# Half-column matrix products of a gated-linear-attention and a state-space layer, gathered into one row per head and per group

## The chip, the cores and the metric

One core of a Trainium2 chip runs the whole kernel in one launch. The metric is the device time of one execution in microseconds, the median of three runs. One more execution was recorded by the hardware profiler; all rows below come from it.

## The reference, cut to what matters

Two layers work on 1024 tokens of width 1024 in float32. Each has an RMS norm in front, one wide input projection, a token mixer, a SiLU gate, an output projection and a residual add.

Layer 0 (GLA) has 4 heads, key width 128, value width 512. With `b` the running sum of the log gates inside a chunk it computes

```
attn = sum(q[i] * k[j] * exp(b[i] - b[j]))        # j <= i, over the 128 key channels
o    = (q * exp(b)) @ S  +  attn @ v
S    = exp(b_last) * S   +  (k * exp(b_last - b)).T @ v
```

Layer 1 (SSD, Mamba-2) has 8 groups of 4 heads of 64 columns and a state of 128; with `a` the running sum of decays

```
y = ((C @ B.T) * exp(a[l] - a[s])) @ xdt  +  (C @ h) * exp(a)  +  x * D      # s <= l
h = exp(a_last) * h + B.T @ (xdt * exp(a_last - a))
```

Gate and norm follow in both (`o = rmsnorm(o) * silu(g)`; `y = rmsnorm(y * silu(z))`), and a last norm ends the trunk.

## The kernel before

Time is cut into two blocks of 512 tokens; the program runs GLA block 0, GLA block 1, SSD block 0, SSD block 1. A chunk inside a block is 128 tokens, so a block has four (`NC`). Wide projections are done in three `fp32r` products (high by high, high by low, low by high; lines 223 to 225, and 468 to 470 for the values). They are cut into units of 12 products of 512 columns; every unit needs a piece of weight, cast by ScalarE (line 171) and, at its first use, split by GpSimd (line 176), which is the case in block 0 of either layer.

Beside the units run side programs, the mixers, one per head or group. They are Python generators; after every unit a mixer is moved on by about one `yield`. This gives a priority; a scheduler then sets each engine's final order from a timeline of its own. The order is fixed once built: on the chip an engine that reaches an instruction whose data are late stops there.

The GLA mixer of a head makes `attn` in pieces, with exponents that stay small: products at three scales `s` of 16, 4 and 1 rows, and one of 64 rows. `keys(s)` and `queries(s, ...)` (lines 574 to 604) build the scaled operands on VectorE and ScalarE, two halves per scale. `products` (line 606) multiplies them, the two halves of a chunk into PSUM partitions 0 to 63 and 64 to 127: each product uses 64 of TensorE's 128 columns. `place` (line 617) copies the parts into `a64` by masks, from there they go to `at`, and line 699 multiplies `at` by `v`. Line 640 is the 64-row product. The operand of the gate has 96 rows, three copies of 32 (lines 429 to 432), and line 539 multiplies it with `wup`, also 96 rows.

The SSD mixer of a group has four heads in two halves `i`. `decays` and `exps` (lines 909 and 923) make the decay matrices `M` on ScalarE, two lines on VectorE multiply them by `cbm` (lines 1033 and 1060), and `outputs(i, M)` (line 931) makes `po` from the carried state (line 936, all 128 columns) and `py` from `xdt` and `M` (line 941, 64 columns each: head 0 of a half into partitions 0 to 63, head 1 into 64 to 127). `gated` reads both from PSUM. `M` and the broadcast decays share six buffers (`v`). Line 268, in the small projections `gk` and `dt`, uses 32 of the columns.

An `fp32` product of these lines leaves two records in the trace, an `fp32r` product one: the 8 products of a half in line 941 are `x16`.

PSUM has four banks for projections (`pp`) and four for mixers (`mb`). Engine names: `V` VectorE (DVE), `A` ScalarE (ACT), `G` GpSimd (POOL), `PE` TensorE.

Of the kernel before, what the change touches and what calls it, by code (L numbers as in the profile page):

```python
# [10 lines left out]
F32 = mybir.dt.float32  # L11
# [5 lines left out]
P = 128  # L17
# [36 lines left out]
def hybrid_kernel(ctx: ExitStack, tc: tile.TileContext, xT, w_in0, w_gk, w_up, w_out0,  # L54
# [16 lines left out]
    def tl(tag, bufs, shape=(P, T), dt=F32):  # L71
        cnt[0] += 1
        return sb.tile(list(shape), dt, name=f"{tag}_{cnt[0]}", tag=tag, bufs=bufs)
# [335 lines left out]
    class Gla:  # L409
# [13 lines left out]
        def gk(self):  # L423
            def evac(o):

                low = o
                if self.raw:
                    V.tensor_tensor(low, o, self.r[0][0:32, :], op=ALU.mult)
                st = tl("stp", 2, (96, T), F32R)
                V.tensor_copy(st[0:32, :], low)  # L430
                V.tensor_tensor(st[32:64, :], low, st[0:32, :].bitcast(F32), op=ALU.subtract)
                V.tensor_copy(st[64:96, :], low)
                self.low = st[:]
            small_units(w_gk, self.rh, self.rl, evac)
# [89 lines left out]
        def mixer(self, h):  # L524
            t = self.t
            q, k = self.q[h], self.k[h]
            wraw = tl("wupr", 1, (96, P))
            dma(wraw[:], w_up[:, h * P:(h + 1) * P])

            wup = tl("wup", 2, (96, P), F32R)  # L530
            V.tensor_copy(wup[:], wraw[:])
# [50 lines left out]

            def queries(s, half):


                w, n = 4 * s, 2 * P // (4 * s)
                own = 4 if s == 1 else 0
                e = tmp() if s == 4 else tl("raw", 2, (P, N_RAW))[:]
                e = e[:, 0:n * (6 * s + own)].rearrange("p (n w) -> p n w", n=n)
                cs = slice(half * 2 * P, (half + 1) * 2 * P)  # L590
                bv, qv = c3(b[:, cs], w), c3(q[:, cs], w)
                after = []
                for i in range(3):
                    f, l = (i + 1) * s, 4 * s
                    o = sum(4 * s - (m + 1) * s for m in range(i))
                    after.append((e[:, :, o:o + l - f], f))
                    V.tensor_tensor(after[-1][0], bv[:, :, f:l], bv[:, :, f - 1:f].to_broadcast([P, n, l - f]),  # L597
                                    op=ALU.subtract)
                act(e[:, :, 0:6 * s], e[:, :, 0:6 * s], AF.Exp, scale=1.0 / 16)
                for o, f in after:  # L600
                    V.tensor_tensor(o, qv[:, :, f:4 * s], o, op=ALU.mult)
                if own:
                    G.tensor_copy(e[:, :, 6:10], qv)
                return e.rearrange("p n w -> p (n w)")

            def products(kk, qq, c0=0):
                p = ps("mb")
                w = qq[0].shape[1] // 4
                for c in range(2 * len(qq)):
                    for hh in range(2):  # L610
                        n = 2 * (c % 2) + hh
                        ks = (c0 + c) * P + hh * 64
                        PE.matmul(p[hh * 64:hh * 64 + 64, c * w:(c + 1) * w], kk[:, ks:ks + 64],  # L613
                                  qq[c // 2][:, n * w:(n + 1) * w], start=True, stop=True)
                return p[:, 0:2 * len(qq) * w]

# [18 lines left out]
            for c in range(NC):  # L635
                cs = slice(c * P, (c + 1) * P)
                PE.transpose(ptk[:, cs], kd[:, cs], ident[:])
            p64 = ps("mb")
            for c in range(NC):
                PE.matmul(p64[0:64, c * 64:(c + 1) * 64], d[:, c * P:c * P + 64], d[:, c * P + 64:(c + 1) * P],  # L640
                          start=True, stop=True)
            k16, q16 = keys(16), [queries(16, i) for i in range(2)]
            yield
            kh, kl = tl("ktok", 1, dt=F32R)[:], tl("t", NTMP, dt=F32R)[:]
            A.copy(kh, ptk[:])
            V.tensor_tensor(kl, ptk[:], kh.bitcast(F32), op=ALU.subtract)
            A.copy(at[0:64, :, 64:P], c3(p64[0:64, 0:NC * 64], 64))
            yield
# [9 lines left out]

            p16 = products(k16, q16)
            k4, q4 = keys(4), [queries(4, i) for i in range(2)]  # L660
            yield
            q1 = [queries(1, 0)]
            place(16, p16)
            p4 = products(k4, q4)
            yield
            p1 = [products(k, q1)]
            q1 = [queries(1, 1)]
            place(4, p4)
            yield
            place(1, p1[0], 0, 2)  # L670
            p1.append(products(k, q1, 2))
            yield
            place(1, p1[1], 2, 4)
            A.copy(at[0:64, :, 0:64], a64[0:64, :, :])
# [4 lines left out]

            o2 = [tl(tag, 1, (P, 2, T))[:] for tag in ("o0", "o1")]  # L680
            o = [o2[vb // 2][:, vb % 2, :] for vb in range(4)]
# [60 lines left out]
    class Ssd:  # L742
# [10 lines left out]
        def steps(self):  # L753
# [26 lines left out]
            dma(a_cum[self.t][:], ac)  # L780
            acs = tl("stp", 2, (96, T), F32R)[0:64, :]
            self.acs = acs
# [111 lines left out]
        def mixer(self, g):  # L894
# [15 lines left out]
            def decays(i, CD):  # L910
                M = []
                for hh in range(2):
                    h = 4 * g + 2 * i + hh
                    m = tl("v", 6)[:]
                    for c in range(NC):
# [14 lines left out]

            def outputs(i, M):
                po, py = ps("mb"), ps("mb")
                for c in range(NC):
                    cs = slice(c * P, (c + 1) * P)
                    if H[c] is not None:
                        last = PE.matmul(po[:, cs], H[c][:, i * P:(i + 1) * P], Ct[:, cs], start=True, stop=True)  # L936
                for c in range(NC):
                    cs = slice(c * P, (c + 1) * P)
                    for hh in range(2):
                        fs = slice((2 * i + hh) * 64, (2 * i + hh + 1) * 64)  # L940
                        m = PE.matmul(py[hh * 64:(hh + 1) * 64, cs], xdt[:, c, fs], M[hh][:, cs],  # L941
                                      start=True, stop=True)

                        tc.add_manual_dep(m.ins, last.ins.name, ORDER, reason="columns")
                        last = m
                return po, py

# [88 lines left out]
            for c in range(nst):  # L1036
# [9 lines left out]
                if c == NC - 1:  # L1046
                    dma(H_carry[g][:], Hn)
            yield
            py0 = outputs(0, M)
            M = decays(1, CD1)  # L1050
            yield
            exps(M, CD1)
            if end:
                for s in Z:
                    act(s, s, AF.Silu)
            y0 = gated(0, py0, CD)
            yield
            operand(0, y0)
            for hh in range(2):
                V.tensor_tensor(M[hh], M[hh], cbm, op=ALU.mult)  # L1060
            yield
            py1 = outputs(1, M)
            if t and g == SG - 1:
# [3 lines left out]
            yield  # L1067
            y1 = gated(1, py1, CD1)
            yield
# [247 lines left out]
def _layout(i):  # L1317
# [17 lines left out]
    u = f["gla_gate_up"][0]  # L1335
    a["w_up"] = np.concatenate([u, np.zeros_like(u)] * 3, 0)

# [53 lines left out]
```

## Time and profile before

| | |
|---|---|
| median of three runs | 1646.9 us (1645.06 to 1651.49) |
| the profiled execution | 1649.23 us |
| its span, first to last instruction | 1647.4 us |
| TensorE busy / its granted clock, mean | 1601.0 us (97%) / 0.991 |
| VectorE, ScalarE, GpSimd busy | 61%, 58%, 42% |

A product is pipelined: the record of one of 512 columns lasts 0.39 us, but the next begins 0.23 us after it. What a product costs is therefore read from start to start in the timeline, not from its length.

### The profile page before, as it was taken

The numbers are of one execution on the slowest core, as the hardware profiler recorded it, in microseconds if no ns is written. First come the engines' busy times: TensorE is split into PE (matmuls) and PEld (weight loads), VectorE is DVE, ScalarE is ACT, GpSimd is POOL, SyncE is SP. The second block draws the span as 40 slices with busy tenths as digits, with TensorE's granted clock in tenths as the row PEclk, the third lists the DMA queues.
The fourth block names the chain that finished last, engine by engine and source line by source line (L and its number), as shares of the span: only waits on it lengthen the run. The fifth ranks groups of instructions, "written<-read, shape, count | busy, mean of one in ns | idle before, by whom it ended". The sixth has DMA issues, their size and how long they took to land.

```text
span 1647.4 us, 24170 instructions
## 1 busy us (share of the span) xinstructions
PE 1601.0 (97%) x8272; PEld 1310.5 (80%) x8272; DVE 1006.3 (61%) x1675; ACT 950.1 (58%) x1796; POOL 688.0 (42%) x540
## 2 busy tenths in 40 slices
PE   7999899989999999999999999999999999999997
PEld 5777787878888887878887888888778888888886
DVE  6457578595645546376755634466976863355647
ACT  4435364543735365464775757656746777667743
POOL 5457465553322121126535656565434222222323
PEclk9999899999999999999999999999999999999999
DMA  7545456364686456464576566656756776655762
GB/s 235 178 135 154 129 166 201 121 206 150 193 268 190 150 176 208 147 206 128 168 241 217 182 200 187 187 185 215 232 172 199 237 231 211 209 182 182 245 200 84
DMA packets 172492, 309.18 MB, mean 188 GB/s; under 512 B 19089, under 2 KB 24849, under 8 KB 172369
## 3 DMA queue, kind: packets, MB, share of 16 engines
q1 hardware_dynamic: 172368, 307.64, 59.0%
q8 instruction: 65, 1.06, 0.3%
q14 instruction: 59, 0.48, 0.1%
HBM read 231.93 MB, written 75.63 MB: 187 GB/s over the span
## 4 chain that ended last, share of the span: by engine, by line
PE 76%; DVE 15%; ACT 3%; DMA 3%; issue 1%; POOL 1%; SPq 0%; DVEq 0%; ACTq 0%; POOLq 0%
PE pp L223 19%; PE pp L225 18%; PE pp L224 18%; PE pp L468 2%; PE pp L469 2%; PE pp L470 2%; PE mb L941 2%; PE mb L699 2%; PE mb L698 2%; DVE t L731 1%; PE mb L936 1%; PE mb L613 1%; DVE raw L597 1%; PE mb L224 1%; PE mb L223 1%
## 5 line engine op out<-in xcount | busy, mean ns | idle before, releaser
L171 ACT CAST wh<-wraw 128x512 fp32r<-128x512 f32 x472 | 288.7, 617 | 408.7 <-PE pp L224 237.2
L223 PE MATMUL pp<-hh,wh 128*128 128x512 f32 x1184 | 470.2, 398 | 8.6 <-ACT wh L171 7.4
L224 PE MATMUL pp<-hl,wh 128*128 128x512 f32 x1184 | 465.9, 394 | 0.5 <-DVE hl L371 0.5
L225 PE MATMUL pp<-hh,wl 128*128 128x512 f32 x1184 | 464.7, 393 | 0.5 <-POOL wl L176 0.5
L176 POOL TENSOR_TENSOR wl<-wraw,wh 128x512 fp32r<-128x512 f32 x240 | 334.4, 1401 | 290.0 <-ACT wh L171 239.5
L223 PEld LDWEIGHTS pp<-hh,wh 128*128 128x128 f32 x1184 | 223.2, 189 | 60.3 <-ACT wh L171 9.0
L225 PEld LDWEIGHTS pp<-hh,wl 128*128 128x128 f32 x1184 | 223.1, 188 | 48.4 <-issue 2.2
L224 PEld LDWEIGHTS pp<-hl,wh 128*128 128x128 f32 x1184 | 223.4, 189 | 47.9 <-issue 2.9
L223 PE MATMUL pp<-yh,wh 128*128 128x512 f32 x448 | 180.4, 403 | 2.2 <-ACT raw L98 2.2
L225 PE MATMUL pp<-yh,wl 128*128 128x512 f32 x448 | 178.4, 398 | 2.4 <-POOL wl L176 2.4
L224 PE MATMUL pp<-yl,wh 128*128 128x512 f32 x448 | 176.9, 395 | 0.0
L321 POOL TENSOR_TENSOR ss<-ss,t 128x512 f32<-128x512 f32 x53 | 72.7, 1372 | 133.3 <-ACT t L320 132.3
L817 DVE SCALAR_TENSOR_TENSOR m<-pp,pr,m 128x509 f32<-128x509 f32 (+2 forms) x96 | 71.3, 743 | 88.8 <-ACT m L814 87.8
L225 PEld LDWEIGHTS pp<-yh,wl 128*128 128x128 f32 x448 | 84.8, 189 | 23.1 <-POOL wl L176 2.9
L223 PEld LDWEIGHTS pp<-yh,wh 128*128 128x128 f32 x448 | 84.8, 189 | 22.5 <-ACT raw L98 2.6
L468 PE MATMUL pp<-wh,hh 128*128 128x512 f32 x256 | 100.1, 393 | 2.6 <-DVE m L443 2.6
L469 PE MATMUL pp<-wl,hh 128*128 128x512 f32 x256 | 100.4, 392 | 0.0
L470 PE MATMUL pp<-wh,hl 128*128 128x512 f32 x256 | 99.4, 392 | 0.0
L224 PEld LDWEIGHTS pp<-yl,wh 128*128 128x128 f32 x448 | 84.8, 189 | 17.9 <-issue 0.6
L917 ACT ACTIVATE v<-v,tok 128x128 f32<-128x128 f32 x256 | 82.3, 391 | 21.5 <-PE mb L941 18.6
L954 POOL TENSOR_TENSOR t<-t,v 128x384 f32<-128x384 f32 (+1 forms) x32 | 41.7, 1304 | 117.2 <-DVE t L952 106.9
L817 DVE SCALAR_TENSOR_TENSOR x<-pp,pr,x 128x509 f32<-128x509 f32 (+2 forms) x96 | 71.5, 745 | 29.7 <-ACT x L814 26.4
(281 smaller groups left out, 2694.3 us busy)
## 6 DMA issues: line engine op xcount, KB each, us to landing
wraw<-w_in SPq DMA_DIRECT2D x352, 256.0 KB, 3.5
low_in<-wl SPq DMA_DIRECT2D x176, 256.0 KB, 3.8
wl<-low_in SPq DMA_DIRECT2D x176, 256.0 KB, 3.0
wraw<-w_out SPq DMA_DIRECT2D x128, 256.0 KB, 3.4
low_out<-wl SPq DMA_DIRECT2D x64, 256.0 KB, 4.1
v<-a_cum SPq DMA_DIRECT2D x64, 256.0 KB, 4.2
wl<-low_out SPq DMA_DIRECT2D x56, 256.0 KB, 3.1
xn<-x SPq DMA_DIRECT2D x43, 256.0 KB, 3.9
```

What stands on the lines that cost most here:

```text
L171: A.copy(hi[:, 0:w], raws[n][:, 0:w])
L176: G.tensor_tensor(lo[:, 0:w], raws[n][:, 0:w], hi[:, 0:w].bitcast(F32), op=ALU.subtract)
L223: PE.matmul(o, lh, rh, start=first, stop=False)
L224: PE.matmul(o, lh, rl, start=False, stop=False)
L225: PE.matmul(o, ll, rh, start=False, stop=last)
L321: eng.tensor_tensor(ss, ss, sq, op=ALU.add)
L468: PE.matmul(o, rh[kb][:, cs], wh[:], start=(kb == 0), stop=False)
L469: PE.matmul(o, rh[kb][:, cs], wl[:], start=False, stop=False)
L470: PE.matmul(o, rl[kb][:, cs], wh[:], start=False, stop=(kb == KB - 1))
L817: V.scalar_tensor_tensor(dst[:, s:], o[:, 0:T - s], col(C_CW + j * 32 + si), dst[:, s:], op0=ALU.mult, op1=ALU.add)
L917: A.activation(m[:, cs], CD[hh][:, cs], AF.Relu, bias=tok[:, c, 0, h:h + 1], scale=-1.0)
L954: G.tensor_tensor(y[:, n0:], y[:, n0:], CD[0][:, n0:], op=ALU.add)
```

## The change

In GLA, the products of all scales of a head are issued after the last operand has been built, in one chain of ordered instructions: scale 1 (second half, then first), scale 4, scale 16, the 64-row products. They take four `mb` banks at once (the 64-row parts use free columns of two of them). Scales 16 and 4 get their queries in one piece, in the tiles `o0` and `o1` instead of `raw` and `t`. In SSD, the second half's decays are made before the outputs, in the `raw` tiles, and `outputs` takes both halves: first all of `po`, then all 16 products of `py`. The gate operands get 128 rows, the last 32 of them zero.

```diff
                     V.tensor_tensor(low, o, self.r[0][0:32, :], op=ALU.mult)
-                st = tl("stp", 2, (96, T), F32R)
+                st = tl("stp", 2, (P, T), F32R)
+                G.memset(st[96:P, :].bitcast(F32), 0.0)
                 V.tensor_copy(st[0:32, :], low)
...
             q, k = self.q[h], self.k[h]
-            wraw = tl("wupr", 1, (96, P))
+            wraw = tl("wupr", 1, (P, P))
             dma(wraw[:], w_up[:, h * P:(h + 1) * P])
-            wup = tl("wup", 2, (96, P), F32R)
+            wup = tl("wup", 2, (P, P), F32R)
             V.tensor_copy(wup[:], wraw[:])
...
-            def queries(s, half):
-                w, n = 4 * s, 2 * P // (4 * s)
+            def queries(s, e, c0=0, c1=NC):
+                w, n = 4 * s, (c1 - c0) * P // (4 * s)
                 own = 4 if s == 1 else 0
-                e = tmp() if s == 4 else tl("raw", 2, (P, N_RAW))[:]
                 e = e[:, 0:n * (6 * s + own)].rearrange("p (n w) -> p n w", n=n)
-                cs = slice(half * 2 * P, (half + 1) * 2 * P)
+                cs = slice(c0 * P, c1 * P)
                 bv, qv = c3(b[:, cs], w), c3(q[:, cs], w)
...
-            def products(kk, qq, c0=0):
-                p = ps("mb")
-                w = qq[0].shape[1] // 4
-                for c in range(2 * len(qq)):
-                    for hh in range(2):
-                        n = 2 * (c % 2) + hh
-                        ks = (c0 + c) * P + hh * 64
-                        PE.matmul(p[hh * 64:hh * 64 + 64, c * w:(c + 1) * w], kk[:, ks:ks + 64],
-                                  qq[c // 2][:, n * w:(n + 1) * w], start=True, stop=True)
-                return p[:, 0:2 * len(qq) * w]
             def place(s, p, c0=0, c1=NC):
...
                 PE.transpose(ptk[:, cs], kd[:, cs], ident[:])
-            p64 = ps("mb")
-            for c in range(NC):
-                PE.matmul(p64[0:64, c * 64:(c + 1) * 64], d[:, c * P:c * P + 64], d[:, c * P + 64:(c + 1) * P],
-                          start=True, stop=True)
-            k16, q16 = keys(16), [queries(16, i) for i in range(2)]
+            o2 = [tl(tag, 1, (P, 2, T))[:] for tag in ("o0", "o1")]
+            flat = [x.rearrange("p n w -> p (n w)") for x in o2]
+            k16, q16 = keys(16), queries(16, flat[0])
             yield
...
             V.tensor_tensor(kl, ptk[:], kh.bitcast(F32), op=ALU.subtract)
-            A.copy(at[0:64, :, 64:P], c3(p64[0:64, 0:NC * 64], 64))
+            yield
+            k4, q4 = keys(4), queries(4, flat[1])
             yield
...
-            p16 = products(k16, q16)
-            k4, q4 = keys(4), [queries(4, i) for i in range(2)]
-            yield
-            q1 = [queries(1, 0)]
+            q1 = [queries(1, tl("raw", 2, (P, N_RAW))[:], 2 * i, 2 * i + 2) for i in range(2)]
+            yield
+            banks = [ps("mb") for _ in range(4)]
+            last = []
+            def half_columns(o, lhsT, rhs):
+                m = PE.matmul(o, lhsT, rhs, start=True, stop=True)
+                if last:
+                    tc.add_manual_dep(m.ins, last[-1].ins.name, ORDER, reason="columns")
+                last.append(m)
+            def products(p, kk, qq, w, c0, c1):
+                for c in range(c0, c1):
+                    for hh in range(2):
+                        ks, qs, o = c * P + hh * 64, (2 * (c - c0) + hh) * w, (c - c0) * w
+                        half_columns(p[hh * 64:hh * 64 + 64, o:o + w], kk[:, ks:ks + 64], qq[:, qs:qs + w])
+                return p[:, 0:(c1 - c0) * w]
+            p1 = [products(banks[i], k, q1[i], 160, 2 * i, 2 * i + 2) for i in (1, 0)]
+            p4 = products(banks[2], k4, q4, 96, 0, NC)
+            p16 = products(banks[3], k16, q16, 96, 0, NC)
+            p64 = [banks[2 + c // 2][0:64, 384 + c % 2 * 64:448 + c % 2 * 64] for c in range(NC)]
+            for c in range(NC):
+                half_columns(p64[c], d[:, c * P:c * P + 64], d[:, c * P + 64:(c + 1) * P])
+            yield
+            place(1, p1[0], 2, 4)
+            place(1, p1[1], 0, 2)
+            yield
+            place(4, p4)
+            for i in range(2):
+                A.copy(at[0:64, 2 * i:2 * i + 2, 64:P], c3(banks[2 + i][0:64, 384:512], 64))
+            yield
             place(16, p16)
-            p4 = products(k4, q4)
-            yield
-            p1 = [products(k, q1)]
-            q1 = [queries(1, 1)]
-            place(4, p4)
-            yield
-            place(1, p1[0], 0, 2)
-            p1.append(products(k, q1, 2))
-            yield
-            place(1, p1[1], 2, 4)
             A.copy(at[0:64, :, 0:64], a64[0:64, :, :])
...
-            o2 = [tl(tag, 1, (P, 2, T))[:] for tag in ("o0", "o1")]
             o = [o2[vb // 2][:, vb % 2, :] for vb in range(4)]
...
             dma(a_cum[self.t][:], ac)
-            acs = tl("stp", 2, (96, T), F32R)[0:64, :]
+            acs = tl("stp", 2, (P, T), F32R)[0:64, :]
             self.acs = acs
...
                     h = 4 * g + 2 * i + hh
-                    m = tl("v", 6)[:]
+                    m = tl("raw", 2, (P, N_RAW))[:, 0:T] if i else tl("v", 6)[:]
                     for c in range(NC):
...
-            def outputs(i, M):
-                po, py = ps("mb"), ps("mb")
-                for c in range(NC):
-                    cs = slice(c * P, (c + 1) * P)
-                    if H[c] is not None:
-                        last = PE.matmul(po[:, cs], H[c][:, i * P:(i + 1) * P], Ct[:, cs], start=True, stop=True)
-                for c in range(NC):
-                    cs = slice(c * P, (c + 1) * P)
-                    for hh in range(2):
-                        fs = slice((2 * i + hh) * 64, (2 * i + hh + 1) * 64)
-                        m = PE.matmul(py[hh * 64:(hh + 1) * 64, cs], xdt[:, c, fs], M[hh][:, cs],
-                                      start=True, stop=True)
-                        tc.add_manual_dep(m.ins, last.ins.name, ORDER, reason="columns")
-                        last = m
-                return po, py
+            def outputs(Ms):
+                p = [(ps("mb"), ps("mb")) for _ in Ms]
+                for i in range(len(Ms)):
+                    for c in range(NC):
+                        cs = slice(c * P, (c + 1) * P)
+                        if H[c] is not None:
+                            last = PE.matmul(p[i][0][:, cs], H[c][:, i * P:(i + 1) * P], Ct[:, cs],
+                                             start=True, stop=True)
+                for i in reversed(range(len(Ms))):
+                    for c in range(NC):
+                        cs = slice(c * P, (c + 1) * P)
+                        for hh in (1, 0):
+                            fs = slice((2 * i + hh) * 64, (2 * i + hh + 1) * 64)
+                            m = PE.matmul(p[i][1][hh * 64:(hh + 1) * 64, cs], xdt[:, c, fs], Ms[i][hh][:, cs],
+                                          start=True, stop=True)
+                            tc.add_manual_dep(m.ins, last.ins.name, ORDER, reason="columns")
+                            last = m
+                return p
...
                     dma(H_carry[g][:], Hn)
-            yield
-            py0 = outputs(0, M)
-            M = decays(1, CD1)
-            yield
-            exps(M, CD1)
+            M1 = decays(1, CD1)
+            yield
+            exps(M1, CD1)
             if end:
...
                     act(s, s, AF.Silu)
-            y0 = gated(0, py0, CD)
-            yield
-            operand(0, y0)
+            yield
             for hh in range(2):
-                V.tensor_tensor(M[hh], M[hh], cbm, op=ALU.mult)
-            yield
-            py1 = outputs(1, M)
+                V.tensor_tensor(M1[hh], M1[hh], cbm, op=ALU.mult)
+            yield
+            p = outputs((M, M1))
+            yield
+            y1 = gated(1, p[1], CD1)
+            yield
+            y0 = gated(0, p[0], CD)
             if t and g == SG - 1:
...
             yield
-            y1 = gated(1, py1, CD1)
+            operand(0, y0)
             yield
...
             if g == SG - 1:
```

On TensorE, in the second group of SSD block 0, the half-column products `py` (line 941; `mb` their bank, `v` the decay matrices, `o` is `xdt`) stand in three pieces before:

```order
L936 MATMUL mb_8641<-m_1718_7918,Hw_8614 128x128
L941 MATMUL mb_8642<-v_8450,o_1837_8528 64x128
L941 MATMUL mb_8642<-v_8455,o_1837_8528 64x128
...
L223 MATMUL pp_8672<-hh_1582_7269,wh_8578 128x512
L224 MATMUL pp_8672<-hl_1583_7270,wh_8578 128x512
L225 MATMUL pp_8672<-hh_1582_7269,wl_8579 128x512
L936 MATMUL mb_8729<-m_1718_7918,Hw_8614 128x128
L941 MATMUL mb_8730<-v_8654,o_1837_8528 64x128
L223 MATMUL pp_8750<-hh_1521_7052,wh_8621 128x512
...
L225 MATMUL pp_8750<-hh_1544_7142,wl_8622 128x512
L941 MATMUL mb_8730<-v_8659,o_1837_8528 64x128
```

and now in one, the second half (`raw`) first:

```order
L225 MATMUL pp_8521<-hh_1537_7108,wl_8437 128x512
...
L946 MATMUL mb_8564<-m_1678_7776,Hw_8472 128x128
L953 MATMUL mb_8565<-raw_8484,o_1797_8386 64x128
L953 MATMUL mb_8565<-raw_8479,o_1797_8386 64x128
...
L953 MATMUL mb_8563<-v_8313,o_1797_8386 64x128
L953 MATMUL mb_8563<-v_8308,o_1797_8386 64x128
```

Pieces of 8, 1 and 7 products with projections between them became one of 16. Of the 16 groups, 15 have three pieces before and one piece now; the seventh of block 0 has 8 and 8 in both. The eight products of line 268 in SSD block 1 stood in four pieces, one of them against a piece of line 941, and stand in two.

On VectorE, in the same group, the multiplications that complete the decay matrices (`v` the first half's, `raw` the second's) before:

```order
L1033 TENSOR_TENSOR v_8450<-v_8450,m_1829_8490 128x512
L1033 TENSOR_TENSOR v_8455<-v_8455,m_1829_8490 128x512
L1060 TENSOR_TENSOR v_8654<-v_8654,m_1829_8490 128x512
L1009 TENSOR_TENSOR t_8493<-mb_8441,ktok_8492 128x512
...
L1044 TENSOR_TENSOR Hw_8617<-Hw_8617,mb_8563 128x256
...
L1060 TENSOR_TENSOR v_8659<-v_8659,m_1829_8490 128x512
```

and now:

```order
L1044 TENSOR_TENSOR v_8308<-v_8308,m_1789_8348 128x512
L1044 TENSOR_TENSOR v_8313<-v_8313,m_1789_8348 128x512
L1067 TENSOR_TENSOR raw_8479<-raw_8479,m_1789_8348 128x512
L1067 TENSOR_TENSOR raw_8484<-raw_8484,m_1789_8348 128x512
L1020 TENSOR_TENSOR t_8351<-mb_8299,ktok_8350 128x512
```

The last of the four stood behind the state's last update (`Hw`), since its buffer was free only after the first half's outputs; it now stands ahead of the state.

On TensorE, in the second head of GLA block 1, the half-column products (lines 640 and 613; `x4` are four equal rows) before:

```order
L637 MATMUL mb_5164<-ident,t_5112 128x128 x4
L640 MATMUL mb_5169<-t_5137 64x64 x4
L223 MATMUL pp_5149<-hh_763_3643,wh_5089 128x512
...
L613 MATMUL mb_5238<-raw_5178,t_5174 64x96 x4
L613 MATMUL mb_5238<-raw_5186,t_5174 64x96 x4
...
L613 MATMUL mb_5299<-t_5251,t_5247 64x96 x4
L613 MATMUL mb_5299<-t_5259,t_5247 64x96 x4
...
L613 MATMUL mb_5328<-raw_5287,m_1017_4787 64x160 x4
...
L613 MATMUL mb_5369<-raw_5333,m_1017_4787 64x160 x4
```

and now:

```order
L225 MATMUL pp_5192<-yh_4965,wl_5095 128x512
L655 MATMUL mb_5207<-raw_5177,m_992_4697 64x160 x4
L655 MATMUL mb_5206<-raw_5168,m_992_4697 64x160 x4
L655 MATMUL mb_5208<-o_1086_5082,t_5137 64x96 x8
L655 MATMUL mb_5209<-o_1085_5081,t_5083 64x96 x8
L655 MATMUL mb_5208<-t_5049 64x64 x2
L655 MATMUL mb_5209<-t_5049 64x64 x2
L223 MATMUL pp_5244<-yh_4871,wh_5116 128x512
```

Five pieces became one. That is so for six heads; the first two heads of block 0 had two pieces and have two. Over the program TensorE's pieces of 64 or 32 columns go from 88 to 32, with the same 7332 products.

## Rows read from the trace of the kernel before

**Rows 1.** The page, part 1: busy us, share of the span, instructions.
```profile
PE 1601.0 (97%) x8272; PEld 1310.5 (80%) x8272; DVE 1006.3 (61%) x1675; ACT 950.1 (58%) x1796; POOL 688.0 (42%) x540
```

**Rows 2.** The waits of TensorE, whole span: us in total, times, longest.
```profile
PE mb L613 <- DVE raw L601: 7.2, 6, 2.4
PE mb L613 <- DVE t L601: 4.3, 3, 2.9
```

**Rows 3.** Timeline of TensorE, second group of SSD block 0: start, length, records.
```profile
892.97 0.39 PE L936 MATMUL mb<-m,Hw 128*128 128x128 f32 x2
893.28 1.09 PE L941 MATMUL mb<-v,o 128*64 128x128 f32 x16
894.30 0.50 PE L224 MATMUL pp<-hl,wh 128*128 128x512 f32 x1
...
897.38 0.39 PE L225 MATMUL pp<-hh,wl 128*128 128x512 f32 x1
897.61 0.83 PE L936 MATMUL mb<-m,Hw 128*128 128x128 f32 x6
898.37 0.43 PE L941 MATMUL mb<-v,o 128*64 128x128 f32 x2
898.73 0.50 PE L223 MATMUL pp<-hh,wh 128*128 128x512 f32 x1
...
901.36 0.39 PE L225 MATMUL pp<-hh,wl 128*128 128x512 f32 x1
901.68 1.09 PE L941 MATMUL mb<-v,o 128*64 128x128 f32 x14
902.69 0.50 PE L223 MATMUL pp<-hh,wh 128*128 128x512 f32 x1
```

**Rows 4.** Timeline of TensorE, 4 and 8 scale-4 products of two GLA heads.
```profile
260.39 0.40 PE L225 MATMUL pp<-yh,wl 128*128 128x512 f32 x1
260.71 0.55 PE L613 MATMUL mb<-t,t 128*64 128x96 f32 x8
261.19 0.50 PE L223 MATMUL pp<-yh,wh 128*128 128x512 f32 x1
...
456.13 0.40 PE L225 MATMUL pp<-yh,wl 128*128 128x512 f32 x1
456.46 0.88 PE L613 MATMUL mb<-t,t 128*64 128x96 f32 x16
457.27 0.51 PE L223 MATMUL pp<-yh,wh 128*128 128x512 f32 x1
```

**Rows 5.** Timeline of TensorE, one of the four pieces of line 268.
```profile
1195.03 0.40 PE L225 MATMUL pp<-hh,wl 128*128 128x512 f32 x1
1195.36 1.05 PE L268 MATMUL pp<-t,w 128*32 128x512 f32 x4
1196.34 0.50 PE L223 MATMUL pp<-hh,wh 128*128 128x512 f32 x1
```

**Rows 6.** Timeline of TensorE, a gate product of 96 rows and its neighbour.
```profile
426.53 0.40 PE L539 MATMUL mb<-stp,wup 96*128 96x512 f32 x1
426.76 0.40 PE L223 MATMUL pp<-hh,wh 128*128 128x512 f32 x1
```

**Rows 7.** GpSimd's groups of instructions, a fill: busy us, mean ns, idle before.
```profile
L129 POOL MEMSET at<- 128x512 f32 x1 | 0.6, 611 | 0.0
```

**Rows 8.** Timeline, second head of GLA block 0: gate product, VectorE's first and last operand.
```profile
133.21 0.40 PE L539 MATMUL mb<-stp,wup 96*128 96x512 f32 x1
...
146.56 1.86 DVE L550 TENSOR_TENSOR_SCAN m<-t,t 128x128 f32<-128x128 f32 x4
...
177.79 0.78 DVE L601 TENSOR_TENSOR raw<-m,raw 128x192 f32<-128x192 f32 x3
```

**Rows 9.** Windows: span, busy us (instructions) of PE, PEld, DVE, ACT, POOL; clock; DMA.
```profile
170.00:185.00 15.00, 9.78 (x51) 7.29 (x52) 13.31 (x37) 5.29 (x10) 7.56 (x5) 0.66 0.43 140
```

**Rows 10.** Timeline of VectorE, the second half's last decay matrix, group of Rows 3.
```profile
898.03 1.54 DVE L1060 TENSOR_TENSOR v<-v,m 128x512 f32<-128x512 f32 x1 [1.33 <-ACT v L98]
```

More of the change, by code (lines that the diff above doesn't have):

```diff
@@ L1335, in _layout @@
     u = f["gla_gate_up"][0]
-    a["w_up"] = np.concatenate([u, np.zeros_like(u)] * 3, 0)
+    a["w_up"] = np.concatenate([u, np.zeros_like(u)] * 3 + [np.zeros_like(u)] * 2, 0)
     def outw(wo):
```

## The prediction

> **What bounds the kernel now.** I read the page first, then the waits of TensorE, then its timeline around the lines that the change touches, last the other engines there. The page shows TensorE busy for 1601.0 of 1647.4 us, with no other engine above 61% [rows 1]: over the program it is the bound, so what counts is how many steps TensorE makes, how long each is, and where it stands still. The longest waits at the products that move are 7.2 and 4.3 us, on the operands that VectorE builds [rows 2]; I place them by the timeline in GLA block 0. Everywhere else in the stretches below a product starts as soon as the one ahead lets it. The timeline therefore gives prices, from start to start. A full product of 512 columns takes 0.23 (897.38 to 897.61) [rows 3, 6].
>
> **The price of a piece.** Read the three pieces of an SSD group [rows 3]. The step into one is 0.32 (901.36 to 901.68), 0.09 over a full step. A line-936 product in front takes 0.31 (892.97 to 893.28), so without that 0.22. The piece of 8 then costs 892.97 to 894.30 less 0.22 = 1.11; the piece of 7, 901.36 to 902.69 less 0.23 = 1.10; the single product, 897.61 to 898.73 less three times 0.22 = 0.46. Seven cost what eight do: head 0's and head 1's products, in different columns, run beside each other, and an odd one costs as much as a pair. With f for the piece and p for the pair, f + 4p = 1.11 and f + p = 0.46, so p = 0.217 and f = 0.24. The GLA pieces give f again: four 96-wide products cost 260.39 to 261.19 less 0.23 = 0.57, eight 456.13 to 457.27 less 0.23 = 0.91 [rows 4]; so 0.17 a pair, and f = 0.57 - 0.34 = 0.23.
>
> **SSD.** A group's pieces of 8, 1 and 7 cost 3f + 9p, one of 16 costs f + 8p: saved 2f + p = 0.70. 15 groups change (the seventh of block 0 has 8 and 8 in both): 10.4 us. This supposes that a piece of 16 pays f once; the piece of eight pairs is not in the trace, but that of four is, and if it paid f twice, the group would save 0.46 and the term be 6.9.
>
> **GLA.** In six heads five pieces become one: 4f = 0.94 each, 5.6 us; heads 0 and 1 have two pieces in both. The four 64-row products stay unpaired as before.
>
> **Line 268.** One of its pieces costs 1195.03 to 1196.34 less 0.23 = 1.08 [rows 5]; four pieces make 4.3. Two pieces of four products cost 2.2 if the 32-column products run beside each other as the 64-column ones do, and 4 x 0.84 + 2 x 0.24 = 3.8 if each pair keeps its 0.84. Saved 0.5 to 2.1; I take 2.0, near the upper end, since [rows 3] shows products in different columns sharing their time.
>
> **128-row gates.** A 96-row product steps 0.23 to its neighbour [rows 6], as a full one does: 0 of the eight is left to be saved. The Trainium skill, TensorEngine Tiling (Array Packing), Tiling Modes, says that a change of tiling mode drains TensorE, and lists modes of 128, 64 and 32 rows; were 96 such a mode, eight gates would give eight times f, 1.9 us more, and the time would be 1627. The step of 0.23 shows no drain, so I leave it out. The change adds two fills of 32 rows and 512 elements on GpSimd, one for each block; the 128-row fill took 0.61 [rows 7], so at most 1.2, and down to 0 beside GpSimd's own idle time. I take 0.
>
> **Waits in GLA.** Now all products of a head stand behind the last operand. That is the one place where the change can give something back, and it matters in block 0, where TensorE already stands waiting. Take head 1: TensorE comes past its gate at 133.21, VectorE's scan is at 146.56, the last operand starts at 177.79, with TensorE held up at each piece [rows 8]; in that stretch TensorE is busy for 9.78 of 15 us and the granted clock 0.66 [rows 9], part of it thus at 1.2 instead of 2.4 GHz. By the order some 125 products of 0.23 stand between gate and row: TensorE could be there at 133.21 + 28.5 = 161.7. VectorE needs 59 instructions before and 39 larger ones now to the last query; its 59 take 177.79 - 146.56 = 31.2, 0.53 each, so 39 of that size make 20.6 and the row is ready at 167; as some are twice as large, up to 174. So a single wait of 5 to 12 us, against about 9 in several pieces before. The other heads of block 0: head 0 about 2 us worse, head 3 about 2 better, from the same count. One long wait may also hold the clock low longer: the stretch in [rows 9] lost 5 us against the clock 1.00. I take 0 for all four heads, with bounds of -8 (the waits of 11.5 in [rows 2] nearly gone, since VectorE has 12 instructions less per head) to +12. In block 1 the operands come from a VectorE that is not late; nothing waits at these lines there before.
>
> **Waits in SSD.** The second half's decay matrix ends at 898.03 + 1.54 = 899.57 [rows 10], 2.1 ahead of its piece at 901.68, but 6.3 behind the first half's at 893.28 [rows 3]. Had it to be ready at the first half's place, TensorE would wait. But its buffers change from `v`, free only after the first half's outputs, to `raw`, and in VectorE's new order its multiplication stands directly behind the first half's, ahead of the state's update. What stood between goes behind, and the first half was early. I take 0. Four banks of `mb` are held at once by the outputs; behind them the next group's first `mb` product has at least 22 full steps (5 us) by the order, so VectorE's two readers of a pair of banks, estimated at the 1.54 of [rows 10] each, nearly fit: 0, at most 3 in the two tight places. The exponents on ScalarE come earlier by as much as the matrices; ScalarE is busy 58% [rows 1], which covers them.
>
> **Sum.** 10.4 + 5.6 + 2.0 = 18.0, with 0 for the rest. The profiled execution took 1649.23 with a span of 1647.4, 1.8 around it; span 1629.4, execution 1631.2. It lay 2.3 above the median of 1646.9, so the median comes to 1628.9; I say 1629.
>
> **Rivals.** (1) Heads of block 0 are later: one wait per head, longer than the several before, with the clock at 0.66 behind it. For it: VectorE is at 13.31 of 15 us in [rows 9]. Against: it has fewer instructions than before. At +10: 1639. (2) They are earlier, as fewer instructions and one wait instead of six would have it: -8, so 1621. (3) The pieces give back nothing, as the switch stays as dear per product in a longer piece, or the saved time is waited for elsewhere: 1647. Against it stand the equal prices of f in [rows 3, 4]. (4) The slower one: the merged row waits for the second half's matrix at each of 16 groups, because ScalarE's exponents for it do not come earlier, or the buffers `raw` are not free. Were it as late as [rows 10] have it against 893.28, that is 6.3 x 16 = 101, less 18: 1730. It outweighs the gain from 18.0/16 = 1.1 us a group on, and passes 0.5% above from 1.6 (26 us). For it: the matrix was only 2.1 early. Against: its place in VectorE's order ahead of the state.
>
> **How the numbers follow.** A measurement of this kernel can tell about 0.5%, 8.2 us, from no change: faster is below 1638.7, slower above 1655.1. Forecast 0.68 (own range 1624 to 1635), earlier heads 0.08, later heads 0.13, nothing given 0.05, slower 0.06. Faster: 0.68 + 0.08 + 0.08 of the later heads (those below +10) = 0.84. Same: 0.05 + 0.05 = 0.10. Slower: 0.06. The range goes from 1620 to 1641: it leaves out the two last cases, 0.11, and the outer parts of the two before.
>
> **What would show it.** In the new profile a merged SSD row should start after its last line of projections in a step of 0.32, last from start to the next full product about 1.9, and have no idle time in front; a GLA row of block 1 some 3.1 from start to next, without idle; TensorE's busy time should fall by about 15 to 18. A wait on `raw` ahead of the merged row, above 1 us, shows rival 4; waits at the GLA row in block 0 of together more than 20 show rival 1, of less than 6 rival 2; a merged row of 2.2 instead of 1.98 with its step shows f paid twice. My forecast is wrong if the median leaves 1620 to 1641, or lies inside with the terms not those above.

## The result and the profile after

The changed kernel took 1632.99 us (median of 4, 1624.62 to 1635.6) against 1647.75, the median of four executions of the kernel before: 14.8 us less. The ratio, taken over all executions of both, is 0.9898, 95% interval 0.9876 to 0.9921: 13 to 20 us less, some 17 in the middle. Below, differences in us are what such ratios make of before's time, unless medians are named; the two ways can differ by 2 us. The forecast was 1629, range 1620 to 1641. Measured once more beside later experiments the changed kernel took 1631.08, ratio 0.9892 (0.987 to 0.9914). The profiled execution lasted 1634.13 with a span of 1632.4, 15.0 less than before's span, where 18.0 were forecast.

The page after, same columns as [rows 1]:

```profile
PE 1580.0 (97%) x8272; PEld 1308.2 (80%) x8272; DVE 984.5 (60%) x1579; ACT 947.2 (58%) x1788; POOL 692.8 (42%) x542
```

TensorE is busy 21.0 us less, where 15 to 18 were forecast, with as many products, but the span is only 15.0 shorter: TensorE now stands still 6.0 longer. Both halves of that are in the rows. First the shorter steps: the timeline of TensorE (start, length, records) at a gate as in [rows 6], a GLA head of block 1, the SSD group of [rows 3], and a piece of line 268 as in [rows 5]:

```profile
421.44 0.39 PE L471 MATMUL pp<-wh,hl 128*128 128x512 f32 x1
421.67 0.39 PE L540 MATMUL mb<-stp,wup 128*128 128x512 f32 x1
...
453.09 0.40 PE L225 MATMUL pp<-yh,wl 128*128 128x512 f32 x1
453.42 1.31 PE L655 MATMUL mb<-raw,m 128*64 128x160 f32 x16
454.55 1.49 PE L655 MATMUL mb<-o,t 128*64 128x96 f32 x32
455.87 0.63 PE L655 MATMUL mb<-t 128*64 128x64 f32 x8
456.43 0.50 PE L223 MATMUL pp<-yh,wh 128*128 128x512 f32 x1
...
886.67 0.83 PE L946 MATMUL mb<-m,Hw 128*128 128x128 f32 x6
887.44 1.09 PE L953 MATMUL mb<-raw,o 128*64 128x128 f32 x16
888.36 1.04 PE L953 MATMUL mb<-v,o 128*64 128x128 f32 x16
889.33 0.50 PE L223 MATMUL pp<-hh,wh 128*128 128x512 f32 x1
889.67 0.39 PE L224 MATMUL pp<-hl,wh 128*128 128x512 f32 x1
...
1186.07 1.07 PE L268 MATMUL pp<-t,w 128*32 128x512 f32 x8
1187.06 0.50 PE L223 MATMUL pp<-hh,wh 128*128 128x512 f32 x1
```

The SSD piece of 16 costs 886.67 to 889.33 less three products of 0.22, 2.00, where f + 8p said 1.98: f is paid once. The GLA row takes 453.42 to 456.43, 3.01, and 0.09 for the step in (3.1 forecast), with no idle time in front. Four products of line 268 cost 1187.06 - 1186.07 + 0.09 = 1.08, no more than two did: the upper end of the bound. The 128-row gate comes 0.23 behind its neighbour, as the 96-row one did (426.31 to 426.53 before).

One step was left out of the price. The first full product behind a piece steps 0.34 to the next (889.33 to 889.67) instead of 0.23, and so it did before, behind the product at 902.69 in [rows 3]:

```profile
903.03 0.40 PE L224 MATMUL pp<-hl,wh 128*128 128x512 f32 x1
```

So a piece costs another 0.11 behind the 0.24.

Now the standing still. The waits of TensorE, in GLA block 0 (0 to 400 us), then in GLA block 1 (400 to 790), then in SSD block 0 (800 to 1200); us in total, times, longest:

```profile
PE pp L223 <- ACT wh L171: 7.5, 2, 7.0
PE pp L225 <- POOL wl L176: 4.6, 1, 4.6
PE mb L655 <- DVE raw L601: 3.4, 1, 3.4
PE pp L469 <- DVE m L444: 2.7, 1, 2.7
PE mb L626 <- DVE t L560: 2.4, 2, 1.4
PE pp L223 <- DVE sg L419: 2.4, 2, 2.0
PE pp L223 <- DVE acc L515: 1.7, 2, 1.3
...
PE mb L655 <- DVE t L581: 0.5, 1, 0.5
...
PE pp L223 <- DVE v L480: 4.2, 3, 1.4
...
PE mb L223 <- ACT o L1033: 1.4, 1, 1.4
PE mb L946 <- DVE Hw L1055: 1.4, 1, 1.4
PE mb L224 <- POOL t L1035: 1.3, 2, 0.9
PE pp L223 <- ACT acc L883: 1.1, 2, 0.6
PE mb L953 <- DVE Hw L1055: 0.6, 1, 0.6
...
```

The same view of before, GLA block 1 and SSD block 0:

```profile
PE pp L223 <- DVE v L479: 1.2, 3, 0.4
...
PE mb L223 <- ACT o L1022: 1.7, 2, 0.9
PE pp L225 <- POOL wl L176: 0.5, 1, 0.5
PE mb L224 <- POOL t L1024: 0.3, 2, 0.2
```

In block 0 the 11.5 us on lines 613 [rows 2] shrank to 3.9 on line 655, but projections wait for other results of VectorE and GpSimd instead; without the first product's wait for its weights (6.9 before, 7.0 after), all waits over 0.05 us there add up to 21.0 after 23.6. In GLA block 1 they rose from 1.2 to 4.8, in SSD block 0 from 2.6 to 6.8, in SSD block 1 they stayed at 1.6. So waits took back 5.2 net of the 18.0 us, and 18.0 - 5.2 = 12.8 were to come, against 15.0 in the spans. In GLA block 1, from line 268 at its start to line 268 behind it, the stretch went from 371.26 to 369.56 us although the waits rose by 3.6: TensorE's steps there are 5.3 shorter, not 4 x 0.94 = 3.8. The 16 pieces fewer at the 0.11 left out make 1.8, so this covers the 1.5 between. In the SSD layer the steps shrank by 13.4 where 12.4 were forecast; 30 pieces fewer would have given 3.3 more, so some of it went elsewhere, and I can't say where. Beside that, two executions differ by as much: with the gates alone changed, a run whose median equals before's, one profiled span was 1644.2, 3.2 under before's.

### The profile page after: what moved, and what is told of

The parts are those of the page before. It is cut to its first block, busy times and chain, and to the rows that moved or that the text cites. A ratio compares the mean times of both kernels' runs of the same rounds, so it can differ in the third digit from the quotient of the medians.

```text
span 1632.4 us, 23995 instructions
## 1 busy us (share of the span) xinstructions
PE 1580.0 (97%) x8272; PEld 1308.2 (80%) x8272; DVE 984.5 (60%) x1579; ACT 947.2 (58%) x1788; POOL 692.8 (42%) x542
## 4 chain that ended last, share of the span: by engine, by line
PE 78%; DVE 11%; ACT 4%; DMA 3%; issue 2%; POOL 2%; SPq 0%; DVEq 0%; ACTq 0%; POOLq 0%
PE pp L223 19%; PE pp L225 19%; PE pp L224 19%; PE pp L469 3%; PE pp L470 3%; PE pp L471 3%; PE mb L953 2%; PE mb L706 2%; DMA wraw<-w_in 2%; PE mb L705 2%; PE mb L946 1%; PE mb L655 1%; POOL wl L176 1%; PE mb L224 1%; PE mb L223 1%
## 5 line engine op out<-in xcount | busy, mean ns | idle before, releaser
L176 POOL TENSOR_TENSOR wl<-wraw,wh 128x512 fp32r<-128x512 f32 x240 | 352.6, 1478 | 268.6 <-ACT wh L171 233.7
L645 POOL TENSOR_TENSOR t<-v,t 128x512 fp32r<-128x512 f32 x28 | 40.6, 1460 | 101.5 <-ACT t L644 65.7
L739 POOL TENSOR_TENSOR t<-t,sg 128x512 f32<-128x512 f32 x32 | 50.9, 1621 | 75.3 <-ACT sg L98 68.3
```

Of the source, the lines that this page charges most:

```text
L176: G.tensor_tensor(lo[:, 0:w], raws[n][:, 0:w], hi[:, 0:w].bitcast(F32), op=ALU.subtract)
L645: G.tensor_tensor(vl, v[c], vh.bitcast(F32), op=ALU.subtract)
L739: G.tensor_tensor(u, u, self.g[h][vb], op=ALU.mult)
```

## The experiments

Theory: the pieces are worth what the prices say (f a piece, p a pair), and the new waits are of two kinds, one with the GLA rows in block 1, one with the SSD rows in block 0. First each part by itself. **SSD alone** (the diff's edits to `decays`, `outputs` and the mixer's end).

> Only the SSD part of the change is made: one piece of 16 per group, GLA and gates as before. By the prices of the prediction (0.24 us a piece, 0.217 a pair) TensorE's steps get 15 x 0.69 = 10.4 us shorter and line 268 another 2.0: 12.4. The profile of the whole change shows 4.7 us of new waits of TensorE in SSD block 0 (after 1.4 before). If these come from the merged SSD rows, they are here too, and the kernel is about 8 us faster than before (ratio 0.995). If they come from elsewhere, the full 12 (ratio 0.9925). A rival that holds the piece's price for nothing and the gain for one of other order: 0 to 3 us.

Measured: 1639.81, ratio 0.9958 (0.9945 to 0.9972), 6.9 us faster. That is near the 8 expected; the full 12 lie outside the interval. Its rows of 16 cost 1.99 each, line 268 goes into two pieces, and the waits of SSD block 0 add up to 6.9 us (with the GLA part alone, below, to none): they belong to the merged rows. In SSD block 1 they are 3.5, after 1.6.

**GLA alone** (the edits to `queries`, `products` and the head's mixer).

> Only the GLA part: one row per head, SSD and gates as before. Prices: 6 heads x 0.94 = 5.6 us less. Theory: block 0 gains a little beside it (waits 2.6 us less in the profile of the whole change), block 1 loses 3.6 us to new waits on line 480 (VectorE's copies of the values): together 4 to 5 us faster than before, ratio 0.997. Rival: the waits of block 1 and the slower clock in block 0 take it all back: 0 +- 1.5.

Measured: 1639.29, ratio 0.9956 (0.9943 to 0.997), 7.2 us, more than the 4 to 5 expected: the step left out gives some of that, and in SSD block 0, which this run doesn't touch, there is no wait above 0.05 after 2.6 before. In block 1 the heads cost 3.11 (steps in and out included) and the waits on the values' copies are the same 4.2. The two parts' 6.9 and 7.2 make up the whole within their intervals (14.1 against some 17 by the ratios, 16.5 against 14.8 by the medians).

**Gates alone** (128 rows).

> Only the gate part: operands of 128 rows. The step of 0.23 us to a 96-row product says 0: the same time within 1 us. The rival, a drain at a change of row tiling, makes it 1.9 us faster (eight times 0.24). In the trace the step into and out of a gate product tells it exactly: 0.23 either way by the first, 0.23 now against more before by the second.

Measured: 1647.48, ratio 0.9999 (0.9988 to 1.0009). Nothing, as the step said. The interval leaves room for a gain of up to 2 us, so it doesn't exclude the rival's 1.9 by itself; the steps do. Into and out of the 128-row product they are 0.23, as with 96 rows:

```profile
424.30 0.39 PE L471 MATMUL pp<-wh,hl 128*128 128x512 f32 x1
424.52 0.39 PE L540 MATMUL mb<-stp,wup 128*128 128x512 f32 x1
424.75 0.39 PE L223 MATMUL pp<-hh,wh 128*128 128x512 f32 x1
```

**One piece more per group:** the changed kernel with the second half's `po` and `py` first, then the first half's.

```diff
-                for i in range(len(Ms)):          # all po, then all py
+                for i in reversed(range(len(Ms))):    # po(i), then py(i)
                     for c in range(NC):
                         if H[c] is not None:
-                            last = PE.matmul(p[i][0][:, cs], ...)
+                            step(PE.matmul(p[i][0][:, cs], ...))
-                for i in reversed(range(len(Ms))):
                     for c in range(NC):
                         for hh in (1, 0):
```

> The changed kernel, but each group's 16 products in two pieces of 8, with the three or four full products of the other half's po between them, in one ordered chain. Nothing else in the code differs. One piece more in 15 groups: 15 x 0.24 = 3.6 us; line 268 falls back to four pieces in this order, 2.0: 5.6 slower than the changed kernel, so about 1638 to 1639. In the trace a piece of 8 costs 1.11 (with its steps in and out) against 1.99 for 16. Rival: what was saved was the odd product and the projections between, not the switch: then 8 + 8 costs what 16 does, and only line 268's 2.0 are lost.

Measured: 1635.78, ratio 0.9934 (0.992 to 0.9948) against 0.9892 and 0.9898 of the changed kernel: 6 to 7 us slower by the ratios, 3 to 5 by the medians. The intervals are about 2 and 4 us to either side, so the times alone hardly tell 5.6 from 2.0; the timeline does:

```profile
886.04 0.83 PE L953 MATMUL mb<-m,Hw 128*128 128x128 f32 x6
886.80 1.09 PE L959 MATMUL mb<-raw,o 128*64 128x128 f32 x16
887.82 0.94 PE L953 MATMUL mb<-m,Hw 128*128 128x128 f32 x6
888.68 1.09 PE L959 MATMUL mb<-v,o 128*64 128x128 f32 x16
889.71 0.50 PE L223 MATMUL pp<-hh,wh 128*128 128x512 f32 x1
```

886.04 to 889.71 is 3.67; less six products of 0.22 the two pieces cost 2.35 against 2.00, 0.24 of it the second f. The other 0.11 is the step behind a piece: the three products of line 953 (`x6`) last 0.83 in front of the first piece and 0.94 right behind it. So 8 + 8 cost more than 16, and the switch itself is what was saved. Line 268 stands in four pieces again, as expected; waits in SSD block 0 are 2.8 instead of 6.8.

**No products side by side.** In the merged row `for hh` was put outside `for c`.

> The changed kernel, but in the merged SSD rows the four products of one head of a half stand together, then the four of the other: still one piece of 16, but no product beside one that uses the other 64 columns. Theory of pairs: each then costs the 0.217 of a pair alone, a row 0.24 + 16 x 0.217 = 3.7 instead of 1.99: 16 x 1.74 = 28 us slower than the changed kernel, so 1661. Rival: the price is 0.109 a product however they stand (and an odd product costs more for another reason): no change.

Measured: 1637.85, ratio 0.9936 (0.9924 to 0.9949): some 7 us slower than the changed kernel, neither 28 nor 0. One row of it:

```profile
886.27 1.25 PE L953 MATMUL mb<-raw,o 128*64 128x128 f32 x13
887.26 0.32 PE L953 MATMUL mb<-v,o 128*64 128x128 f32 x1
887.36 0.27 PE L953 MATMUL mb<-raw,o 128*64 128x128 f32 x1
...
887.64 1.20 PE L953 MATMUL mb<-v,o 128*64 128x128 f32 x13
888.77 0.50 PE L223 MATMUL pp<-hh,wh 128*128 128x512 f32 x1
```

886.27 to 888.77 is 2.50 against 1.89 (887.44 to 889.33): 16 x 0.61 = 9.8 us, part of which smaller waits gave back (3.2 us instead of 6.8 in SSD block 0). Records of `v` begin while `raw` still runs, so products in different columns overlap without being neighbours in the order. My theory of pairs was too strict.

Next the waits. VectorE multiplies four decay matrices in a row now; the two new ones, ahead of the state's operands, take 2.4 us together at 869.32, and 1.2 to 3.4 where they stand in a row in other groups. **State first:** an order on VectorE.

```diff
-                V.tensor_tensor(M1[hh], M1[hh], cbm, op=ALU.mult)
+                m = V.tensor_tensor(M1[hh], M1[hh], cbm, op=ALU.mult)
+                tc.add_manual_dep(m.ins, xs.ins.name, ORDER, reason="state first")
```

> The changed kernel with one more order on VectorE: the second half's two multiplications with cbm (line 1067) stand behind the last operand of the state (line 1028) instead of ahead of it. Theory: TensorE's new waits in SSD block 0 (line 223 on o of line 1033, 224 on t of line 1035, 946 and 953 on Hw of line 1055, in all some 5 us) come from the 2.4 us by which these two multiplications hold up the state's operands; they go, less 1.0 us because line 268 falls into three pieces in this order: 3 to 4 us faster than the changed kernel, ratio to before about 0.9885. Rival: the multiplications were not what held the state up, or the merged row now waits for them instead: the same as the changed kernel or slower, waits of line 953 on raw in the trace.

Measured: 1632.33, ratio 0.9899 (0.9886 to 0.9913): the changed kernel's time. The waits on `o` and `t` in SSD block 0 fell from 2.7 to 1.0, but 1.2 came up in block 1, and line 268 fell into three pieces. So the order of these multiplications isn't shown as the main cause. What held `o` at the wait of 1.2 in that run is seen in its timeline of ScalarE, and below it the same at the wait of 1.4 in the changed kernel:

```profile
1549.95 1.28 ACT L924 ACTIVATE raw<-v,tok 128x128 f32<-128x128 f32 x4 [2.07 <-DMA v<-a_cum]
1551.26 0.63 ACT L98 ACTIVATE v<-v 64x512 f32<-64x512 f32 x1
1551.90 0.62 ACT L1033 CAST o<-t 128x512 fp32r<-128x512 f32 x1
```

```profile
919.44 0.62 ACT L171 CAST wh<-wraw 128x512 fp32r<-128x512 f32 x1 [2.33 <-DMA wraw<-w_in]
919.96 0.77 ACT L821 ACTIVATE x<-pp,pr 128x512 f32<-128x512 f32 x1
920.64 0.61 ACT L1033 CAST o<-t 128x512 fp32r<-128x512 f32 x1
```

Both times the cast stands in ScalarE's queue behind an instruction that waits 2.1 or 2.3 us for its DMA; in the changed kernel its operand had been ready since 916.71, as VectorE's row says:

```profile
916.03 0.68 DVE L1028 TENSOR_TENSOR t<-mb,tok 128x512 f32<-128x512 f32 x1
```

That is two waits and not all. In the second profile of the changed kernel, with the same order on every engine, the DMA of that place came earlier and TensorE did not wait there. Its one wait on `o` (1.0) lay a group earlier, behind a cast that had waited for VectorE:

```profile
873.27 0.62 ACT L1033 CAST o<-t 128x512 fp32r<-128x512 f32 x1 [3.07 <-DVE t L1028]
...
917.51 0.62 ACT L171 CAST wh<-wraw 128x512 fp32r<-128x512 f32 x1 [1.00 <-DMA wraw<-w_in]
```

**The cast on VectorE:** `A.copy(hi, xe)` became `V.tensor_copy(hi, xe)`.

> The changed kernel with the cast of the state's operand o (line 1033) on VectorE instead of ScalarE. Theory after the run with the state first: the cast stands in ScalarE's queue behind weight casts and the second half's decays that wait for their DMAs, and TensorE's waits on o and on t (line 1035) come from there: they fall from 2.9 us in SSD block 0 to under 1, less 1.0 us for line 268 in three pieces: 1 to 2 us faster than the changed kernel. Rival: it is VectorE that is late, and the waits stay or grow with one more instruction there: 0 to 3 us slower.

Measured: 1625.96, ratio 0.987 (0.9848 to 0.9893): by ratio and median 4 to 5 us faster than the changed kernel measured beside it (0.987 to 0.9914), with intervals that overlap. Its waits in SSD block 0:

```profile
PE pp L224 <- DVE hl L354: 0.6, 1, 0.6
PE mb L223 <- DVE o L1033: 0.3, 1, 0.3
PE mb L946 <- DVE Hw L1051: 0.2, 1, 0.2
```

Those on `o` and `t` fell from 2.7 to 0.3, those on `Hw` from 2.0 to 0.2. That the cast's queue is the cause isn't shown by this. The scheduler also set other instructions anew; 2.5 us of waits went in GLA block 0, where the order is the changed kernel's; and the next run shows that SSD block 0 can lose most of its waits without the move.

**The values' copies on ScalarE:** without the two lines `elif c % 2: V.tensor_copy(vt, banks[c][:])`, once in the changed kernel, once in the kernel before.

> The changed kernel with all four copies of the values out of PSUM on ScalarE (two stood on VectorE, line 480). Theory: TensorE's three waits of 1.4 us in GLA block 1 are for those copies, which stand behind VectorE's norm chain; they go and the kernel is 3 to 4 us faster than the changed kernel. Rival: ScalarE's copies come as late, or its weight casts then do: the same time.

Measured: 1626.33, ratio 0.9874 (0.9859 to 0.9889). The waits of GLA block 1 fell from 4.8 to 0.9 us. Those of SSD block 0 fell too, from 6.8 (5.7 in the second profile) to 2.2, though every engine's order there is the changed kernel's; in SSD block 1 they rose from 1.6 to 3.1. So part of the waits in SSD block 0 hangs on the timing of an execution, not on the order.

> The kernel before with all copies of the values on ScalarE. Theory: the 4.2 us of waits on them in GLA block 1 are new with the merged rows; before they were 1.2, so at most 1 us is gained here (ratio 0.9994). Rival: the copies' move gains its 5 us whatever the rows are: 1642, ratio 0.997.

Measured: 1647.14, ratio 0.9993 (0.998 to 1.0005): nothing, and not the rival's 5. The gain of the copies' move, and the wait that it ends, are new with the rows.

**Combined.** State first with the values' copies:

> The edits of the two runs before together. If the waits are independent, 6 to 8 us faster than the changed kernel: about 1626, ratio to before 0.9865. If one only hides the other: as the better of the two.

Measured: 1627.27, ratio 0.9876 (0.9861 to 0.9891): as the copies alone, not the 6 to 8 us of two independent gains. The cast and the values' copies moved:

> The values' copies on ScalarE and the cast of o on VectorE together. If both waits go independently: 1624 to 1626. If the cast's move does nothing: line 268's 1.0 slower than with the copies alone, 1627.

Measured: 1623.76, ratio 0.9849 (0.9826 to 0.9873), 7 us under the changed kernel's 1631.08 beside it and faster than both kernels; each of its executions (1620.92 to 1626.5) is faster than each of that kernel's (1629.57 to 1631.68). TensorE still waits 1.9 us on `o` and `t` in SSD block 0, with the cast on VectorE. And that changed kernel:

> The changed kernel once more, as the measure for the runs beside it: 1633, ratio to before 0.990. If the prices of the prediction hold and only waits differ between executions, its pieces again cost 1.99 per SSD group and 3.11 per GLA head in block 1.

Its pieces: 1.99 and 3.11 again, 1631.08.

## Why the prediction came out as it did

- **The prices held, with one step missing.** 2f + p, 4f and line 268's 2.0 were read from rows of before and met the new rows within 0.02 us a piece. The price was read up to the first full product behind a piece; that product's own step, 0.34 instead of 0.23, was left out, so f is 0.35 and not 0.24. That is part of why TensorE's busy time fell by 21.0, and 24.9 in the second profile, and not by 15 to 18. It made up for part of the waits below. Line 268 is tied to the SSD rows: with SSD alone it has two pieces, with GLA alone four.
- **The gates' 0 held**, by the step and by a run of their own.
- **GLA block 0.** The term 0 was fair (waits 2.6 us less), but not by the path forecast: the single wait of 5 to 12 us at head 1's row didn't come. TensorE waited 4.6 on line 225 for GpSimd's split of a weight, ahead of the row, and found the row's operands ready. The test I named for rival 2 misleads: "waits at the GLA row in block 0 ... of less than 6 rival 2". They were 3.9, and the other 8 us forecast by that rival did not come: the wait moved in part to lines 223, 225 and 626, on VectorE and GpSimd. I should have named the waits of the whole stretch.
- **"In block 1 ... nothing waits at these lines"** was true and not enough: 3.6 us of waits arose at line 223, for copies of the values on VectorE, which come later than TensorE now; moving them off VectorE brought these waits down to 0.9.
- **The step that was mis-sized is "What stood between goes behind, and the first half was early. I take 0."** The merged rows themselves never waited for their decays, so rival 4 was rightly low. But TensorE waited 4.2 us more in SSD block 0 (3.1 in the second profile), most of it for the state and its operands (4.7 of the 6.8), and this comes with the merged SSD rows. Why is open in part: the state put first on VectorE gained nothing in time; one wait of 1.4 stood behind a DMA in ScalarE's queue, which its busy share of 58% did not tell, but not so in the second profile. The same order had 6.8, 5.7 and 2.2 us of waits there in three profiles, so no single queue is shown as the cause.
- A median 2 to 4 us above the forecast is these two terms (3.6 and 4.2), less the 2.6 of block 0 and the 2.4 by which TensorE's steps shrank more than forecast. That the sum came so near the forecast is in part luck: the terms left out have opposite signs.

## What to carry to other kernels

A piece of products on part of TensorE's columns has a fixed price beside that of its products; read both from pieces of different lengths in one trace, count the step behind the first full product too, and the gain of merging them follows nearly. What such a merge costs appears at other lines: work that is moved changes when other work is ready, so list what it passes on every engine and who waits for that. After the change look for the new waits. Here those of GLA block 1 went by moving copies from VectorE to ScalarE, and that move did nothing for the kernel before; the move of the cast was not tried there. Before you name a queue as the cause, look at a second profile of the same order: a wait can move or go by itself.

## What the hardware showed that I had not expected

Products in different columns overlap even when several of one column group stand first: with four products of a head together, a row of 16 took 2.50 us where strict pairs took 1.89 and no overlap would have taken 16 x 0.217 = 3.5. Four products of 32 columns cost 1.08 with their steps, as much as two.
